# The router of a transformer block on unnormalised rows, in quarters, and the first experts with fixed rows

## The chip, the core and the metric

The kernel runs on one core of a Trainium2 chip. TensorE (PE) multiplies matrices, VectorE (DVE) and ScalarE (ACT) work on rows and on what PE leaves in its accumulator banks (PSUM), GpSimd (POOL) does simple row operations, and the queue of SyncE (SP) issues most transfers. Each engine works through its own list of instructions in order; semaphores make it wait for the others. The metric is the device time of one execution in microseconds (us); less is better.

## The reference, cut to what matters

One encoder block over 512 tokens of width 1024: differential attention and a short convolution are mixed by gates, then a residual, a LayerNorm, a two-level mixture of experts and a second LayerNorm. The change touches the part from `w_o` to the first experts:

```python
mix = (g_a * y_a + g_b * y_b) @ w_o
x = layer_norm(DEEPNORM_ALPHA * x + mix, ln1_g, ln1_b)
g_prob = softmax(x @ w_group + b_group)            # 4 groups, the best is taken
sub_logits = einsum('td,gde->tge', x, w_sub) + b_sub   # 8 experts in each, the best two
weights = g_p * softmax(s_top)
y_e = (silu(x_e @ w_gate_e[e]) * (x_e @ w_up_e[e])) @ w_down_e[e]   # 32 experts, d_expert 512
x = layer_norm(DEEPNORM_ALPHA * x + sum of weight * y_e, ln2_g, ln2_b)
```

`layer_norm(x, g, b)` is `(x - mean) / sqrt(var + eps) * g + b`. All data is float32. For products of full precision the kernel splits one or both factors into a high and a low part (fp32r) and adds the products.

## The kernel before, in words

The schedule is written out by hand: the order in the source is the order on each engine. Tokens stand in four tiles of 128 (`tt` 0 to 3). SBUF is divided into 22 pages of 1 MB, which are handed out in the order in which their last readers stand in the source.

`o_group(j, tt)` multiplies a token tile by a quarter (256 columns) of `w_o` with 24 matmuls (L286 to L288); DVE adds the residual into `u(tt)` and takes the quarter's statistics (L677, L678). The four quarters of `w_o` are units that are split into parts first (`Unit.split`, L168 on ACT, L169). For the last three units of `w_o` DVE makes the first half of the low part and POOL the second (`prep(..., nc.gpsimd)`).

When a tile's four quarters are done, `layer_norm` normalises it on DVE and applies scale and shift (L107 to L115). `turn_x` transposes the normalised tile on PE (L694) and ACT copies it out (L696); `logits` multiplies it by the 36 router columns (L714); `parts_x` makes `XH` on ACT (L705), `XL` on POOL (L706), and multiplies the tile by alpha on POOL (L708). `gate_steps` is a chain of some 16 small DVE operations from the logits to the table of chosen experts `MEM` (L722 to L757). `rank` (L764 to L766) gives each chosen token its place in its expert's list, `counts` (L793) the length of the lists, `positions` (L777 to L788) the row in the expert's input.

The loop over `NP` = 16 follows. Each `i` stands for two experts (a pair), each `dispatch` for two `i`. `dispatch` compares positions with a row of numbers (L821) and gathers by matmuls with `XH` and `XL` (L905, L906); ACT copies the rows to `XG` (L908, L911). `up(i)` is 8 steps of gate and up products (L944), `act` the nonlinearity, `down` the third product (L971). `combine` adds an earlier pair's rows to `u` (L997 on PE, L999 on DVE). An expert's rows need not be 64: each pair may shift 32 rows from its first to its second expert, which `select` reads from `SEL` into a register of PE. What is over 64 (or 96) rows goes to one expert that is run again at the end.

Weights come by page: `experts.load` issues a page's load on SP when a page is given back, 14 pages ahead of use. Before `up` of the first pair, PE has gathered a half of its input (two of four steps of `dispatch(0)`), and gathers the rest between its steps.

Of the kernel before, what the change touches and what calls it, by code (L numbers as in the profile page):

```python
# [37 lines left out]
def block(ctx: ExitStack, tc, a, out, dump=None, stop=None):  # L38
# [174 lines left out]
    class Experts:  # L213

        def __init__(self):
# [4 lines left out]
            self.order = [(i, kind, n) for i in range(NP)  # L222
# [146 lines left out]
    prm = setup[0:42, 1152:1280]  # L369
# [5 lines left out]
    nc.sync.dma_start(prm[40:42], a["subln_g"].rearrange("o (k p) -> (o k) p", p=128))  # L375
    nc.sync.dma_start(lqk[:, 0], a["lambda_q"])
# [4 lines left out]
    rrow = early.tile([1, 36], F32, name="rrow")  # L381
    nc.gpsimd.dma_start(wr[:, :, 0:4], rows_of(a["w_group"][0]))
# [19 lines left out]
    pcol = early.tile([128, 42], F32, name="pcol")  # L402
    ps = ps_tp.tile([128, 512], F32, name="tp")
    nc.tensor.transpose(ps[:, 0:42], prm, ident[0:42, 0:42])
    nc.scalar.copy(pcol, ps[:, 0:42])
# [170 lines left out]
    onesb = early.tile([128, 128], BF, name="onesb")  # L576
# [11 lines left out]
                   allow_small_or_imprecise_dtypes=True)  # L588
    XH, XL = [], []
# [6 lines left out]
    MEM = early.tile([128, NT, NE], BF, name="mem")  # L596
# [85 lines left out]
    rows, gates = {}, {}  # L682

    def turn_x(tt):

        if tt % 2 == 0:
            XH.append(page(f"xh{tt}", (128, 2, D), F32R))
            XL.append(page(f"xl{tt}", (128, 2, D), F32R))
        x2 = u(tt)
        xt = att.tile([128, KC, 128], F32, name="xt", tag="p", bufs=3)  # L690
        for i in range(2):
            ps = ps_tp.tile([128, 512], F32, name="tp")
            for k in range(4):
                nc.tensor.transpose(ps[:, k * 128:(k + 1) * 128],  # L694
                                    x2[:, (i * 4 + k) * 128:(i * 4 + k + 1) * 128], ident)
            nc.scalar.copy(xt[:, 4 * i:4 * i + 4], ps.rearrange("p (k t) -> p k t", k=4))  # L696
# [615 lines left out]
```

## Time and profile before

| | before |
|---|---|
| median of 3 runs | 1167.73 us (1166.67 to 1167.89) |
| the profiled execution | 1169.97 us, its span 1168.3 us |
| mean granted clock of TensorE | 0.974 |
| busy share of the span | PE 93%, DVE 40%, ACT 23%, POOL 12% |
| bytes moved | 264.89 MB, mean 227 GB/s |

A row of the timeline is: start and duration in us, engine, line and operation, output and inputs, shape, and in brackets how long the engine had been idle and what ended that. The 1.67 us between span and time lie around the profiled instructions. Matmuls overlap, so one lasts longer than the distance to the next. A granted clock of 1.0 is 2.4 GHz, 0.5 is 1.2 GHz.

### The profile page before, as it was taken

The page shows a single profiled execution, that of the slowest core. Times are in us where ns is not written, and L with a number is a line of the kernel's source. Part 1 is how long each engine was busy: PE and PEld are TensorE (multiplying, and loading weights), DVE is VectorE, ACT ScalarE, POOL GpSimd, SP SyncE. Part 2 cuts the span into 40 slices and gives each one's busy share as a digit, 9 for nine tenths or more (in the row PEclk, how much of TensorE's full clock was granted, in tenths as well). Part 3 has the DMA queues.
Part 4 walks back from the last instruction along what each step waited for, and adds up shares of the span by engine and source line. Part 5 has one row for each costly group of instructions (what it writes and reads, how often), then busy time and mean ns, then how long its engine had stood idle before and what let it go on. Part 6 is the DMA issues. An engine that isn't in the chain of part 4 may idle for free. (4 is left out here: it accounts for less than half of the span.)

```text
span 1168.3 us, 17372 instructions
## 1 busy us (share of the span) xinstructions
PE 1088.7 (93%) x7138; PEld 722.7 (62%) x7138; DVE 465.6 (40%) x1020; ACT 271.6 (23%) x478; POOL 135.9 (12%) x117
## 2 busy tenths in 40 slices
PE   5999999989999999999949999999999999999984
PEld 3998877767888888888936443545454545443333
DVE  6621565654344433247881132323232232322326
ACT  3413545743023323323221110111111011110000
POOL 2304322311000000023342000000000000000002
PEclk9999999989999999999969999999999999999997
DMA  9332212122332232343286899999999999999921
GB/s 296 109 118 72 73 37 73 60 68 89 109 109 73 72 109 94 122 143 110 80 352 234 326 408 359 408 402 409 400 409 399 410 406 395 409 407 357 413 79 72
DMA packets 103326, 264.89 MB, mean 227 GB/s; under 512 B 4528, under 2 KB 49644, under 8 KB 102732
## 3 DMA queue, kind: packets, MB, share of 16 engines
q1 hardware_dynamic: 102300, 262.27, 59.9%
q8 instruction: 60, 0.98, 0.3%
q10 hardware_dynamic: 720, 1.31, 0.3%
q0 software_dynamic: 224, 0.15, 0.2%
q14 instruction: 22, 0.18, 0.0%
HBM read 260.30 MB, written 3.41 MB: 226 GB/s over the span
## 5 line engine op out<-in xcount | busy, mean ns | idle before, releaser
L508 PE MATMUL mm<-uth,hi_in 128*128 128x512 f32 x448 | 179.2, 400 | 0.0
L509 PE MATMUL mm<-utl,hi_in 128*128 128x512 f32 x448 | 174.8, 390 | 0.0
L510 PE MATMUL mm<-uth,lo_in 128*128 128x512 f32 x448 | 174.7, 390 | 0.0
L944 PE MATMUL gu<-wg,xg 128*32 128x512 f32 (+1 forms) x1024 | 133.3, 592 | 0.0
L944 PE MATMUL gu<-wu,xg 128*32 128x512 f32 (+1 forms) x1024 | 133.2, 592 | 0.0
L971 PE MATMUL y<-wd,ht 128*32 128x512 f32 (+1 forms) x1024 | 114.9, 601 | 1.4 <-ACT ht L963 1.4
L509 PEld LDWEIGHTS mm<-utl,hi_in 128*128 128x128 f32 x448 | 84.4, 188 | 18.6 <-issue 1.0
L508 PEld LDWEIGHTS mm<-uth,hi_in 128*128 128x128 f32 x448 | 84.4, 188 | 18.4 <-ACT oth L476 0.5
L999 DVE TENSOR_TENSOR u<-u,x 128x512 f32<-128x512 f32 x120 | 75.9, 683 | 49.9 <-PE x L997 49.9
L510 PEld LDWEIGHTS mm<-uth,lo_in 128*128 128x128 f32 x448 | 84.4, 188 | 17.8
L954 DVE SCALAR_TENSOR_TENSOR h<-h,w,gu 128x512 f32<-128x512 f32 x16 | 12.0, 747 | 180.9 <-PE gu L944 180.9
L944 PEld LDWEIGHTS gu<-wu,xg 128*32 128x32 f32 x1024 | 33.1, 110 | 76.8 <-issue 72.6
L944 PEld LDWEIGHTS gu<-wg,xg 128*32 128x32 f32 x1024 | 32.7, 110 | 74.8 <-issue 69.6
L997 PE MATMUL x<-ys,st 128*128 128x512 f32 x240 | 67.1, 405 | 12.3 <-DVE u L999 7.1
L971 PEld LDWEIGHTS y<-wd,ht 128*32 128x32 f32 x1024 | 31.8, 111 | 73.2 <-issue 70.5
L169 POOL TENSOR_TENSOR lo_in<-raw_in,hi_in 128x1024 fp32r<-128x1024 f32 x25 | 59.1, 2384 | 146.9 <-ACT hi_in L168 96.2
L905 PE MATMUL x<-S,xh 128*128 128x256 f32 (+1 forms) x256 | 68.8, 302 | 0.6 <-POOL over L1022 0.6
L168 ACT CAST hi_in<-raw_in 128x1024 fp32r<-128x1024 f32 x64 | 63.6, 1046 | 15.5 <-DVE lo_wa L169 8.9
L906 PE MATMUL x<-S,xl 128*128 128x256 f32 (+1 forms) x256 | 66.2, 292 | 0.0
L980 DVE TENSOR_TENSOR ys<-y,ys 128x512 fp32r<-128x512 f32 x32 | 22.0, 691 | 109.7 <-ACT ys L978 109.7
L169 DVE TENSOR_TENSOR lo_in<-raw_in,hi_in 128x1024 fp32r<-128x1024 f32 x39 | 46.0, 1220 | 46.6 <-ACT hi_in L168 46.5
L997 PEld LDWEIGHTS x<-ys,st 128*128 128x128 f32 x240 | 41.1, 188 | 25.2 <-DVE u L999 13.3
(299 smaller groups left out, 1596.6 us busy)
## 6 DMA issues: line engine op xcount, KB each, us to landing
wg<-in_w_gate_e SPq DMA_DIRECT2D x64, 1024.0 KB, 12.4
wu<-in_w_up_e SPq DMA_DIRECT2D x64, 1024.0 KB, 12.4
wd<-in_w_down_e SPq DMA_DIRECT2D x64, 1024.0 KB, 10.0
raw_in<-in_w_in SPq DMA_DIRECT2D x32, 1024.0 KB, 5.6
raw_wa<-in_w_a_proj SPq DMA_DIRECT2D x4, 1024.0 KB, 5.2
raw_wb<-in_w_b_proj SPq DMA_DIRECT2D x4, 1024.0 KB, 5.0
raw_wo<-in_w_o SPq DMA_DIRECT2D x4, 1024.0 KB, 5.5
u<-in_x SPq DMA_DIRECT2D x4, 512.0 KB, 11.5
```

What stands on the lines that cost most here:

```text
L168: nc.scalar.copy(self.hi[:, k], self.raw[:, k])
L169: eng.tensor_sub(self.lo[:, k], self.raw[:, k], self.hi[:, k].bitcast(F32))
L508: nc.tensor.matmul(ps, unit.hi[:, k, sl], xh(k), start=(k == 0), stop=False)
L509: nc.tensor.matmul(ps, unit.hi[:, k, sl], xl(k), start=False, stop=False)
L510: nc.tensor.matmul(ps, unit.lo[:, k, sl], xh(k), start=False, stop=(k == KC - 1))
L905: nc.tensor.matmul(o, part(XH, tt)[:, sl], r, start=(tt == 0), stop=False)
L906: nc.tensor.matmul(o, part(XL, tt)[:, sl], r, start=False, stop=(tt == NT - 1))
L944: nc.tensor.matmul(t[32 * p:32 * p + 32], disp[i // 2][:, k, base + 32 * p:base + 32 * p + 32], of_rows(w, sel, p), start=(k == 0), stop=( ...
L971: nc.tensor.matmul(Y[hf][32 * p:32 * p + 32], ht[:, f, 32 * p:32 * p + 32], of_rows(w, sel, p), start=(f == 0), stop=(f == 3))
L980: nc.vector.tensor_sub(YS[:, 1, c], y, YS[:, 0, c].bitcast(F32))
L997: nc.tensor.matmul(ps, st[:, tt * 128:(tt + 1) * 128], YS[:, n, c], start=(n == 0), stop=(n == 1))
L999: nc.vector.tensor_add(o, o, ps)
```

## The change

- The router's weights are multiplied by the scale of the first LayerNorm once, early on (`router_weights`), the column sums and the share of the shift go to `wsum` and `rbias`. So `logits` works on the rows before normalisation; `gate_steps` puts mean and deviation in with one more operation.
- `turn_x` and `logits` go by quarters of a tile: a quarter is transposed one `o_group` after its own, and its logits come one later still.
- `norm_x` normalises on ACT without scale and shift; `XL` is made on DVE; scale and shift are applied where gathered rows leave PSUM (`scale_shift`, on ACT, for the first pairs also on DVE). The residual gets scale, shift and alpha in `residual_x` on DVE inside the first pair; POOL multiplies scale and shift (`gb_1`) by alpha once, ahead of the `o_group` loop.
- `rank` and the weights of a tile are asked for later. The loop starts with the pairs 2 and 3 (`sequence`). These have fixed rows, 64 for each expert, so their gather needs ranks alone: `first_slots` and `add_tile` gather tile by tile into four banks that are set to zero first.
- `counts`, `positions`, the transposed positions and the first weights move into `up` of the first pair. Two pages (`XG`, `S0`) are taken ahead of the loop, and one weight page fewer is loaded ahead until the first pair is through.

```diff
+        sequence = [*range(2, NP), 0, 1]
         def __init__(self):
             self.free, self.next, self.tiles = 0, 0, {}
             two = "(h g s) (p k) f -> s h p g k f"
             self.g, self.u = (a[n][0].rearrange(two, h=2, g=2, k=KC) for n in ("w_gate_e", "w_up_e"))
             self.d = a["w_down_e"][0].rearrange("(h g s) (j p) c -> s h p j g c", h=2, g=2, p=128)
-            self.order = [(i, kind, n) for i in range(NP)
+            self.order = [(i, kind, n) for i in self.sequence
                           for kind, n in [(c, n) for n in range(4) for c in "gu"] + [("d", n) for n in range(4)]]
             self.order[-4:] = [("over", c, n) for n in range(2) for c in "gu"] + self.order[-4:] + \
...
-    prm = setup[0:42, 1152:1280]
+    prm = setup[0:58, 1152:1280]
...
+    for i, n in enumerate(("ln1_g", "ln1_b")):
+        nc.sync.dma_start(prm[42 + 8 * i:50 + 8 * i], a[n].rearrange("o (k p) -> (o k) p", p=128))
...
+    xcol = small.tile([128, 2, KC], F32, name="xcol")
+    for i, n in enumerate(("ln1_g", "ln1_b")):
+        nc.gpsimd.dma_start(xcol[:, i], a[n][0].rearrange("(p k) -> p k", k=KC))
...
+    def router_weights():
+        byk = lambda ps: ps[:, 0:288].rearrange("p (k c) -> p c k", c=36)
+        t = att.tile([128, KC, 36], F32, name="wb", tag="p", bufs=3)
+        nc.gpsimd.tensor_tensor(t, wr, pcol[:, 50:58].unsqueeze(2).to_broadcast([128, KC, 36]), op=OP.mult)
+        nc.gpsimd.tensor_tensor(wr, wr, pcol[:, 42:50].unsqueeze(2).to_broadcast([128, KC, 36]), op=OP.mult)
+        for w, to in ((t, None), (wr, wsum)):
+            ps = ps_tp.tile([128, 512], F32, name="tp")
+            nc.tensor.matmul(ps[:, 0:288], ones, w.rearrange("p k c -> p (k c)"))
+            if to is None:
+                nc.vector.reduce_sum(wsum, byk(ps), axis=AX.X)
+                nc.vector.tensor_add(rbias, rbias, wsum)
+            else:
+                nc.vector.reduce_sum(to, byk(ps), axis=AX.X)
+    router_weights()
...
+    rows, gates, norms = {}, {}, {}
+    def turn_x(tt, j):
+        if j == 0:
+            rows[tt] = att.tile([128, KC, 128], F32, name="xt", tag="p", bufs=3)
+        ps = ps_tp.tile([128, 512], F32, name="tp")
+        for k in range(2):
+            nc.tensor.transpose(ps[:, k * 128:(k + 1) * 128],
+                                u(tt)[:, (j * 2 + k) * 128:(j * 2 + k + 1) * 128], ident)
+        nc.scalar.copy(rows[tt][:, 2 * j:2 * j + 2], ps[:, 0:256].rearrange("p (k t) -> p k t", k=2))
+    def logits(tt, j):
+        if j == 0:
+            rows[tt, "logits"] = ps_pv.tile([128, 256], F32, name="pv")
+        for k in range(2 * j, 2 * j + 2):
+            nc.tensor.matmul(rows[tt, "logits"][:, 0:36], rows[tt][:, k, :], wr[:, k, :],
+                             start=(k == 0), stop=(k == KC - 1))
+    def norm_x(tt):
+        steps = norm_steps(stats[tt])
+        mv, rs = next(steps)
+        yield
+        yield from steps
+        nb = work.tile([128, 1], F32, name="ln_nb")
+        nc.vector.scalar_tensor_tensor(nb, mv[:, 0:1], -1.0, rs, op0=OP.mult, op1=OP.mult)
+        norms[tt] = rs, nb
+        yield
+        nc.scalar.activation(u(tt), u(tt), AF.Identity, scale=rs, bias=nb)
+        yield
+    def parts_x(tt):
         if tt % 2 == 0:
             XH.append(page(f"xh{tt}", (128, 2, D), F32R))
             XL.append(page(f"xl{tt}", (128, 2, D), F32R))
-        x2 = u(tt)
-        xt = att.tile([128, KC, 128], F32, name="xt", tag="p", bufs=3)
-        for i in range(2):
-            ps = ps_tp.tile([128, 512], F32, name="tp")
-            for k in range(4):
-                nc.tensor.transpose(ps[:, k * 128:(k + 1) * 128],
-                                    x2[:, (i * 4 + k) * 128:(i * 4 + k + 1) * 128], ident)
-            nc.scalar.copy(xt[:, 4 * i:4 * i + 4], ps.rearrange("p (k t) -> p k t", k=4))
-        rows[tt] = xt
-    def parts_x(tt):
-        x2 = u(tt)
-        xk = x2.rearrange("t (p k) -> t k p", k=KC)
+        xk = u(tt).rearrange("t (p k) -> t k p", k=KC)
         h, l = (part(t, tt).rearrange("t (k p) -> t k p", k=KC) for t in (XH, XL))
         nc.scalar.copy(h, xk)
-        nc.gpsimd.tensor_sub(l, xk, h.bitcast(F32))
-        nc.gpsimd.tensor_scalar(x2, x2, ALPHA, None, op0=OP.mult)
-    def logits(tt):
-        xt = rows[tt]
-        ps = ps_pv.tile([128, 256], F32, name="pv")
-        for k in range(KC):
-            nc.tensor.matmul(ps[:, 0:36], xt[:, k, :], wr[:, k, :], start=(k == 0), stop=(k == KC - 1))
-        rows[tt] = ps[:, 0:36]
+        yield
+        nc.vector.tensor_sub(l, xk, h.bitcast(F32))
+        yield
+    def residual_x(tt):
+        nc.vector.tensor_mul(u(tt), u(tt), g1)
+        nc.vector.tensor_add(u(tt), u(tt), b1)
...
-        nc.vector.tensor_add(L, rows.pop(tt), rbias)
+        rs, nb = norms[tt]
+        nc.vector.scalar_tensor_tensor(L, wsum, nb, rbias, op0=OP.mult, op1=OP.add)
+        yield
+        nc.vector.scalar_tensor_tensor(L, rows[tt, "logits"][:, 0:36], rs, L, op0=OP.mult, op1=OP.add)
...
-        ct = ps_tp.tile([128, 512], F32, name="tp")
+        ct = bank()
...
+        nc.gpsimd.memset(CAP[:, 2 * first:2 * first + 4], 64.0)
...
+    first = experts.sequence[0]
+    XG = page("xg0", (128, KC, 256))
+    S0 = page("s0", (128, NT, 2, 128), F32R)
+    W0 = small.tile([128, 4], F32, name="w0")
+    def first_slots(tt):
+        r = RK[:, tt, 2 * first:2 * first + 4].rearrange("p (i j) -> p i j", j=2)
+        for j, ranks in enumerate((iota2, iota1[:, 0:64])):
+            nc.vector.tensor_tensor(S0[:, tt, :, 64 * j:64 * j + 64], ranks.unsqueeze(1).to_broadcast([128, 2, 64]),
+                                    r[:, :, j:j + 1].to_broadcast([128, 2, 64]), op=OP.is_equal)
+    def dispatch_first():
+        banks = [(ps_lg if i < 2 else ps_mm).tile([128, 512], F32, name="lg" if i < 2 else "mm")
+                 for i in range(4)]
+        for t in banks:
+            nc.tensor.matmul(t, onesb, tri[:, 0:1].to_broadcast([128, 512]), start=True, stop=False)
+        return banks
+    def add_tile(banks, tt):
+        r = S0[:, tt].rearrange("p i s -> p (i s)")
+        for x in (XH, XL):
+            for k in range(KC):
+                o = banks[k // 2][:, (k % 2) * 256:(k % 2) * 256 + 256]
+                end = tt == last and x is XL and k % 2 == 1
+                nc.tensor.matmul(o, part(x, tt)[:, k * 128:(k + 1) * 128], r, start=False, stop=end)
+                if end:
+                    for i in (k - 1, k):
+                        scale_shift(XG[:, i], banks[k // 2][:, (i % 2) * 256:(i % 2) * 256 + 256], i, i % 2)
+    def scale_shift(dst, src, k, vector=False):
+        g, b = xcol[:, 0, k:k + 1], xcol[:, 1, k:k + 1]
+        if vector:
+            nc.vector.tensor_scalar(dst, src, g, b, op0=OP.mult, op1=OP.add)
+        else:
+            nc.scalar.activation(dst, src, AF.Identity, scale=g, bias=b)
     prep(NU, NU - 2, nc.gpsimd)
     experts.load(EARLY)
+    nc.gpsimd.tensor_scalar(gb_1, gb_1, ALPHA, None, op0=OP.mult)
     for tt in range(NT):
         for j in range(4):
             if tt == 0 and j < 2:
                 prep(NU, NU - 1 + j, nc.gpsimd)
             o_group(j, tt)
-            if j == 0 and tt > 1:
-                ratio(tt - 2)
-            if j == 2 and 0 < tt < last:
-                turn_x(tt - 1)
-                parts_x(tt - 1)
-            if j == 2 and tt == last or j == 3 and tt == last - 1:
+            before = 4 * tt + j - 1
+            if before >= 0 and before < 4 * last + 3:
+                turn_x(before // 4, before % 4)
+                if before > 0:
+                    logits((before - 1) // 4, (before - 1) % 4)
+            if tt and j == 0:
+                together(norm_x(tt - 1))
+            if tt and j == 1:
+                cast = parts_x(tt - 1)
+                next(cast)
+                together(gate_steps(tt - 1))
+                ratio(tt - 1)
+                together(cast)
+            if tt > 1 and j == 1:
                 rank(tt - 2)
-            if j == 3 and 0 < tt < last:
-                logits(tt - 1)
-        if tt == last:
-            turn_x(last - 1)
-            parts_x(last - 1)
-            logits(last - 1)
-        layer_norm(u(tt), g1, b1, stats[tt], 4, *([gate_steps(tt - 1)] if 0 < tt < last else []),
-                   *([weight_steps(tt - 2)] if tt > 1 else []))
+                together(weight_steps(tt - 2))
+                first_slots(tt - 2)
     ui += 4
-    experts.load(AHEAD - EARLY)
-    turn_x(last)
-    together(gate_steps(last - 1))
-    logits(last)
-    parts_x(last)
-    ratio(last - 1)
+    experts.load(AHEAD - EARLY - 1)
+    banks = dispatch_first()
+    turn_x(last, 3)
+    add_tile(banks, 0)
+    logits(last, 2)
+    logits(last, 3)
+    together(norm_x(last))
+    add_tile(banks, 1)
     rank(last - 1)
-    together(gate_steps(last), weight_steps(last - 1))
+    first_slots(last - 1)
+    add_tile(banks, last - 1)
+    cast = parts_x(last)
+    next(cast)
+    together(gate_steps(last))
+    rank(last)
+    first_slots(last)
+    together(cast)
+    add_tile(banks, last)
     ratio(last)
-    counts()
-    rank(last)
-    positions()
+    together(weight_steps(last - 1))
     together(weight_steps(last))
     nc.gpsimd.tensor_add(GP, of_pair(G)[:, :, :, 0], of_pair(G)[:, :, :, 1])
     mix.close()
...
-    disp, weight = {}, {}
+    disp = {first // 2: XG}
+    weight = {first + i: W0[:, 3 * i:3 * i + 1] for i in range(2)}
...
-                nc.scalar.copy(XG[:, k], ps[:, 0:256])
-                nc.scalar.copy(over["x"][:, k], ps[:, 256:320])
+                scale_shift(XG[:, k], o[:, 0:256], k)
+                scale_shift(over["x"][:, k], o[:, 256:320], k)
             elif k % 2:
-                nc.scalar.copy(XG[:, k - 1:k + 1], ps.rearrange("p (k s) -> p k s", k=2))
+                for i in (k - 1, k):
+                    scale_shift(XG[:, i], ps[:, i % 2 * 256:i % 2 * 256 + 256], i)
...
+        if sel is None:
+            return t[:, p // 2]
...
+    coming = None
+    sels = {first: None, first + 1: None}
+    steps = up(first, None)
+    advance(steps, 2)
+    counts()
+    positions()
+    advance(steps, 3)
     POS_T = bank()
     for tt in range(NT):
         nc.tensor.transpose(POS_T[0:NP, tt * 128:(tt + 1) * 128], POS[:, tt], ident)
     nc.scalar.copy(POST, POS_T[0:NP])
-    coming = dispatch(0)
-    advance(coming, 2)
-    sels = {0: select(0)}
-    steps = up(0, sels[0])
-    for _ in range(3):
-        advance(coming, 1)
-        advance(steps, 2)
-    advance(coming)
+    ps = bank()
+    for i in range(2):
+        for tt in range(NT):
+            nc.tensor.matmul(ps[:, 2 * i:2 * i + 2], S0[:, tt, i].bitcast(F32), GP[:, tt, first:first + 2],
+                             start=(tt == 0), stop=(tt == last))
+    nc.scalar.copy(W0, ps[:, 0:4])
     adding = None
-    for i in range(NP):
-        if i % 2 == 0 and i + 2 < NP:
-            coming = dispatch(i // 2 + 1)
+    for n, i in enumerate(experts.sequence):
+        after = experts.sequence[n + 1] if n + 1 < NP else None
+        if n % 2 == 0 and n + 2 < NP:
+            coming = dispatch(experts.sequence[n + 2] // 2)
             advance(coming, 1)
-        if i + 1 < NP:
-            sels[i + 1] = select(i + 1)
+        if after is not None and after not in sels:
+            sels[after] = select(after)
         advance(steps)
         h = act(*GU, weight[i])
-        if i == 0:
+        if n == 0:
+            for tt in range(NT):
+                residual_x(tt)
+            experts.load(1)
```

## Rows read from the trace of the kernel before

**Rows 1.** Busy time by stage; columns as the first line says.

```profile
core 0: us, PE busy (x) PEld busy (x) DVE busy (x) ACT busy (x) POOL busy (x), PEclk, DMA share, GB/s
545.00:587.30 42.30, 40.48 (x340) 39.90 (x339) 34.15 (x109) 8.58 (x13) 11.43 (x4) 1.00 0.29 109
...
591.00:613.40 22.40, 6.90 (x39) 5.75 (x40) 19.70 (x67) 4.63 (x10) 13.70 (x10) 0.51 0.83 333
613.40:619.80 6.40, 6.37 (x32) 6.28 (x32) 0.97 (x3) 0.64 (x2) 4.95 (x19) 0.57 0.01 3
619.80:640.10 20.30, 20.30 (x177) 9.56 (x176) 1.43 (x4) 3.81 (x6) 2.32 (x11) 1.00 0.80 296
640.10:1133.00 492.90, 477.38 (x4006) 219.03 (x4002) 133.03 (x229) 56.50 (x113) 0.95 (x1) 1.00 0.97 381
```

**Rows 2.** Busy time between the last load ahead and the loop's first loads.

```profile
609.50:622.60 13.10, 10.18 (x64) 7.61 (x68) 4.21 (x19) 1.75 (x3) 9.06 (x35) 0.64 0.01 4
```

**Rows 3.** Timeline of PE from the last quarter of `w_o` to the first expert.

```profile
587.24 1.04 PE L694 MATMUL tp<-ident,u 128*128 128x128 f32 x8
588.51 1.98 PE L714 MATMUL pv<-wr,xt 128*128 128x36 f32 x16 [0.24 <-ACT xt L696]
...
608.50 0.19 PE L793 MATMUL tp<-mem,onesb 128*128 128x32 bf16 x1 [6.94 <-DVE mem L756]
...
613.43 0.55 PE L905 MATMUL x<-S,xh 128*128 128x256 f32 x1 [0.59 <-POOL over L1022]
...
619.82 1.06 PE L944 MATMUL gu<-wg,xg 128*32 x8
```

**Rows 4.** Timeline of DVE: first and last operation of two chains.

```profile
545.88 0.26 DVE L107 BATCH_NORM_AGGREGATE ln_mv<-ln_st 128x2 f32<-128x24 f32 x1
...
547.89 0.16 DVE L85 TENSOR_TENSOR ln_rs<-ln_i,ln_t 128x1 f32<-128x1 f32 x1
...
596.82 0.19 DVE L722 TENSOR_TENSOR L<-pv,rbias 128x36 f32<-128x36 f32 x1
...
600.48 0.19 DVE L756 TENSOR_TENSOR mem<-oh,oh 128x32 bf16<-128x32 f32 x1
```

**Rows 5.** Groups of POOL by line: xcount, busy us, mean ns, idle before.

```profile
L706 POOL TENSOR_TENSOR xl<-u,xh 128x1024 fp32r<-128x1024 f32 x4 | 11.8, 2954 | 39.7 <-ACT xh L705 39.7
L708 POOL TENSOR_SCALAR u<-u 128x1024 f32<-128x1024 f32 x4 | 11.5, 2868 | 0.4
...
L169 POOL TENSOR_TENSOR lo_wa<-raw_wa,hi_wa 128x1024 fp32r<-128x1024 f32 x2 | 4.7, 2371 | 16.3 <-issue 16.3
```

**Rows 6.** Timeline of POOL, then of PE, in the first token tile.

```profile
534.24 9.18 POOL L169 TENSOR_TENSOR lo_wo<-raw_wo,hi_wo 128x1024 fp32r<-128x1024 f32 x3 [7.96 <-DMA wu<-in_w_up_e]
...
540.12 0.39 PE L288 MATMUL mm<-lo_wo,mth 128*128 128x256 f32 x1 [0.21 <-POOL lo_wo L169]
```

**Rows 7.** Groups of ACT by line.

```profile
L911 ACT COPY xg<-x 128x512 f32<-128x512 f32 x28 | 16.5, 588 | 81.9 <-PE x L906 81.9
...
L705 ACT CAST xh<-u 128x1024 fp32r<-128x1024 f32 x4 | 8.4, 2102 | 0.0
...
L168 ACT CAST hi_wo<-raw_wo 128x1024 fp32r<-128x1024 f32 x8 | 7.8, 1047 | 0.0
...
L1248 ACT ACTIVATE u<-x,nb,rs 128x512 f32<-128x512 f32 x2 | 1.6, 777 | 8.0 <-DVE nb L1267 4.3 <-DVE u L1255 3.7
```

**Rows 8.** Groups of DVE by line.

```profile
L169 DVE TENSOR_TENSOR lo_wb<-raw_wb,hi_wb 128x1024 fp32r<-128x1024 f32 x8 | 9.4, 1222 | 9.3 <-ACT hi_wb L168 9.3
...
L677 DVE SCALAR_TENSOR_TENSOR u<-u,mm 128x256 f32<-128x256 f32 x16 | 6.6, 412 | 8.4 <-PE mm L288 7.2 <-PE tp L765 1.2
```

**Rows 9.** Busy time of PE at two pauses; then PEclk, DMA share, GB/s.

```profile
1131.80:1134.00 2.20, 0.00 (x0) 1.00 0.03 7
1134.00:1135.00 1.00, 0.00 (x0) 0.64 0.00 0
...
700.00:702.50 2.50, 0.63 (x3) 1.00 1.02 408
```

More of the change, by code (lines that the diff above doesn't have):

```diff
@@ L399, in block @@
     v_group(1, 3)
-    pcol = early.tile([128, 42], F32, name="pcol")
+    pcol = early.tile([128, 58], F32, name="pcol")
     ps = ps_tp.tile([128, 512], F32, name="tp")
-    nc.tensor.transpose(ps[:, 0:42], prm, ident[0:42, 0:42])
-    nc.scalar.copy(pcol, ps[:, 0:42])
+    nc.tensor.transpose(ps[:, 0:58], prm, ident[0:58, 0:58])
+    nc.scalar.copy(pcol, ps[:, 0:58])
     nc.vector.tensor_scalar(pcol[:, 40:42], pcol[:, 40:42], 1.0 - LAM_INIT, None, op0=OP.mult)
@@ L575, in block @@
     tri = early.tile([128, 128], BF, name="tri")
-    onesb = early.tile([128, 128], BF, name="onesb")
+    onesb = small.tile([128, 128], BF, name="onesb")
     nc.gpsimd.memset(onesb, 1.0)
@@ L595, in block @@
     POST = small.tile([NP, S], BF, name="post")
-    MEM = early.tile([128, NT, NE], BF, name="mem")
+    MEM = small.tile([128, NT, NE], BF, name="mem")
     CNT = small.tile([128, NE], F32, name="cnt")
@@ L775, in positions @@
         A, B = of_pair(RK)[:, :, :, 0], of_pair(RK)[:, :, :, 1]
-        ta, tb, tc_, td = (work.tile([128, NT, NP], F32, name=f"pos{i}", bufs=1) for i in range(4))
+        big = mw.tile([128, NT, 384], F32R, name="S", bufs=1).bitcast(F32)
+        ta, tb, tc_, td = (big[:, :, i * NP:(i + 1) * NP] for i in range(4))
         nc.gpsimd.tensor_scalar(ta, A, 32.5, -64.0, op0=OP.is_gt, op1=OP.mult)
@@ L867, in block @@
         dump("g", G.rearrange("p t e -> p (t e)"), 0)
-        dump("pos", POS.rearrange("p t e -> p (t e)"), 0)
-        dump("cnt", CNT, 0)
     mix.close()
@@ L891, in dispatch @@
         disp[j] = XG
-        more = j == NP // 2 - 1
+        more = 2 * j == experts.sequence[-2]
         if more:
@@ L1012, in block @@
     NO = small.tile([1, 1], I32, name="no")
-    OVER = small.tile([128, NT, NE], F32, name="over")
     PASS = small.tile([128, 1], F32, name="pass")
@@ L1054, in next_pass @@
         each = ind.unsqueeze(1).to_broadcast([128, NT, NE])
-        nc.vector.tensor_tensor(big, OVER, each, op=OP.mult)
+        nc.vector.tensor_sub(big, RK, CAP.unsqueeze(1).to_broadcast([128, NT, NE]))
+        nc.vector.tensor_tensor(big, big, each, op=OP.mult)
         nc.vector.reduce_sum(PLACE[:, 0], big, axis=AX.X)
@@ L1124, in other_pass @@
                 nc.tensor.matmul(o, part(XL, tt)[:, sl], SO[:, tt, 0:64], start=False, stop=(tt == NT - 1))
-        nc.scalar.copy(x, ps.rearrange("p (k s) -> p k s", k=KC))
+        for k in range(KC):
+            scale_shift(x[:, k], ps[:, k * 64:(k + 1) * 64], k)
         ht = turn(act(*up_over(x, w), over["w"][:, 0:1]))
@@ L1164, in block @@
                                           skip_runtime_bounds_check_because="the number of an expert")
-        if i:
-            st = rows_of(i - 1)
+        if n:
+            st = rows_of(before)
             adding = combine(st, YS)
-        if i == NP - 1:
+        if n == NP - 1:
             gb_2 = page("gb_2", (128, 2, D))
@@ L1174, in block @@
             advance(adding, 3)
-        if i < NP - 1:
+        if n < NP - 1:
             ht = turn(h)
         advance(adding, 2)
-        if i % 2:
+        before = i
+        if n % 2:
             advance(coming)
-        if i < NP - 1:
+        if n < NP - 1:
             down(i, sels[i], ht)
-        if i == NP - 2:
+        if n == NP - 2:
             npass = nc.values_load(NPASS[0:1, 0:1], min_val=0, max_val=16)
             tc.mark_branch_hint_location("other passes", hint=(npass > 1), engines=[PE])
-        if i < NP - 1:
+        if n < NP - 1:
             YS = parts_y(Y)
-            steps = up(i + 1, sels[i + 1])
-    last_rows = rows_of(NP - 1)
+            steps = up(after, sels[after])
+    last_rows = rows_of(i)
     YO = over["st"][:, 2:4]
@@ L1196, in block @@
         h2 = act(*gu, over["w"][:, 0:1])
-        down(NP - 1, sels[NP - 1], ht)
+        down(i, sels[i], ht)
         y = down_over(turn(h2), over_w)
@@ L1203, in block @@
     with some.Else():
-        down(NP - 1, sels[NP - 1], turn(h))
+        down(i, sels[i], turn(h))
     YS = parts_y(Y)
-    last_rows = rows_of(NP - 1)
+    last_rows = rows_of(i)
     last_banks = [*GU, *(bank() for _ in range(4)), *Y]
```

11 lines of the change are left out of this document (5 added, 6 removed).

## The prediction

> **What bounds the kernel now.** I began with the busy time by stage [rows 1]. Before 587.3 PE is the bound: 40.5 of 42.3 us busy, with DVE close behind (34.2). From 591.0 to 613.4 PE is busy for 6.9 of 22.4 us at a clock of 0.51, while DVE is busy for 19.7: here the router's chain sets the pace. From 619.8 on PE is busy again for 97% of its time.
>
> The timeline of PE says where the gap begins and ends [rows 3]. The last product with `w_o` ends at 587.24, when the transposes of tile 2 start. The wait of 6.94 us ahead of the counts is for `MEM`, the end of DVE's chain. The gather starts at 613.43 and the first expert at 619.82. So 32.6 us lie between the last product with `w_o` and the first expert, and this is what the change is after.
>
> Is an earlier start worth its full time? From 609.5 to 622.6 the transfers stand still (share 0.01) with the weights loaded ahead [rows 2]: the first expert waits for its rows, not its weights. In the loop PE is the busier side (477.4 of 492.9 us, transfers 0.97) [rows 1]. So I count an earlier first expert one for one.
>
> **Part 1, `router_weights`: +1.0 us.** Two f32 products of 288 columns among the matmuls of an earlier stage, where PE has no time to spare. Eight f32 transposes of 128 columns take 1.04 us, so 576 columns take 0.6; an f32 product of the router shows two instructions for each of its 8 steps [rows 3], which makes 1.2. I take 1.0. POOL's two products and DVE's sums run on engines with time to spare; the four more small transfers at the start I put at nothing, and at 1 us if the start waits for them.
>
> **Part 2, alpha times `gb_1` on POOL: +7.8 us.** This stands in POOL's list between the halves of `w_o`'s second and third unit. All of PE's later work is queued behind the product that waits for them. POOL makes three halves in one piece of 9.18 us from 534.24, and PE waits for the second until 540.12 [rows 6]. A tile of 128x1024 times alpha takes POOL 2.87 us [rows 5]; `gb_1` is twice as wide: 5.7 us. The second half would start at some 537.0; with the scaling ahead it starts at 542.7, takes 2.4 (the rate of the halves of `w_a`) and is ready at 545.1, the third at 547.5.
>
> PE has then been idle for some 4.6 us. After 1131.8 a pause of PE took the clock to the lower level (0.64 on average from 1134.0 to 1135.0), a pause of two us at 700 left it [rows 9]; so I take it that it falls. After 613.43 it stayed low for some 5.5 us: a mean of 0.57 over 6.4 us [rows 1]. A matmul comes every 0.12 us at the upper level (340 in 40.5 us), every 0.22 at the lower. From 545.1: 12 matmuls 2.6, a quarter's transposes and logits 1.0, 12 matmuls 2.6, then 12 at the upper level 1.4: 552.7. Before, 12 from about 543.5 end at 544.9. Without the fall it would be +4.9.
>
> **Part 3, tiles 1 to 3: +3.4 us.** PE has 96 matmuls (11.5), eight transposes (1.04) and the logits (1.98 [rows 3]) per tile, 14.5; with all of it inside this stage three tiles are 43.6. DVE has per tile four quarters (0.8 with their statistics; L677 alone is 0.41 [rows 8]), the deviation (2.2 and one operation), the gate chain (3.85 for 16 operations, 0.24 each [rows 4], with the new one 4.1), `XL`, and eight small operations of ranks, weights and slots (1.9).
>
> `XL` on DVE is not in the trace. The same subtraction on rows that lie together takes 1.22 us [rows 8], the lower end. Here the rows are read with a step of 8 elements. ACT takes 2.10 us for such a copy and 1.05 for one without the step [rows 7]; twice 1.22 is 2.44, the upper end. POOL's own ratio for this subtraction is 2.95 to 2.37 [rows 5], which makes 1.5. I take 1.8, between the two. Then DVE has 13.4 us per tile, less than PE, but 7.8 of it (gate, `XL`, small ones) in one piece ahead of the third quarter's eviction. PE can go on for two `o_group`s in that time (7.3 with transposes and logits) before it lacks a bank or a transpose's input; I add 0.7 per tile for that: 45.8. Before it was 42.4 (544.9 to 587.3). The last product now ends at 587.3 + 7.8 + 3.4 = 598.5.
>
> The Trainium skill speaks against this place of the subtraction: "SBUF — State Buffer", section "Door 1: The DMA port swizzle", says that an access which moves on to another line of 16 bytes pays a penalty, and a step of 8 floats does so each time. ACT's rows above agree with it. By that rule alone `XL` is at its upper end, and the sum is 2.5 us more.
>
> **Part 4, from the last product to the first expert: -15.4 us.** What PE and DVE still have to do in turn: wait for the third quarter's eviction 1.3; transposes, logits of a quarter, four matmuls that zero the banks, transposes 1.9; gather of tile 0 (16 matmuls) 1.9; two quarters' logits 1.0; tile 1 1.9; rank, its eviction and slots of tile 2 1.2; gate chain of tile 3 4.1 (the gather of tile 2 beside it); rank and slots 1.2; `XL` 1.8; two matmuls and the copy out 0.8 (an activation of 512 columns takes 0.78 [rows 7], of 256 I take 0.5). Sum 17.1, so the first expert starts at 615.6 instead of 619.8; before, this way took 32.5. What is gone: applying scale and shift on DVE, POOL's subtraction of 2.95 and scaling of 2.87 [rows 5], and the gather of three tiles after the last rank.
>
> **Part 5, inside the first pair: -3.2 us.** Between 619.8 and 640.1 PE still gathers half the input: 32 matmuls, 3.8 us. That is gone. The transposed positions (0.5) and counts (0.2) come in. Positions take DVE and POOL about 3 us after the counts; three steps of `up`, 5.2 us, lie beside them.
>
> **At nothing.** `residual_x`: eight operations on 128x1024, about 1.22 each [rows 8], 9.8 us on DVE right behind the first `act`. PE then has the next gather, a transpose and `down` before DVE's next result is needed; DVE is busy 27% in the loop [rows 1]. Uncovered it would cost its length once. Normalising on ACT (about 1.6) runs beside the gate chain. `XG` and `S0` take two pages, so each load of weights stands two pages, one `o_group`, later; the first expert's weights start when the units of `w_o` are given back, some 12 us ahead of the first expert, and at 381 GB/s [rows 1] a page of 1.05 MB comes every 2.8 us, ahead of its use.
>
> Sum: 1.0 + 7.8 + 3.4 - 15.4 - 3.2 = **-6.4 us**. The profiled execution goes from 1169.97 to 1163.6, the median from 1167.73 to **1161.3**.
>
> **Rivals.**
> *Clock and subtraction kind (25%).* The clock stays up in the first tile (-2.9), or `XL` costs 1.22 (-1.7, since the piece that delays each eviction and the last chain are shorter): 1157 to 1160. For it: the 4.6 us of idling are close to what rows 9 leave open.
> *The subtraction at double price, or the clock low at the first expert (18%).* `XL` at 2.44 adds 2.5. Between the gather of tile 2 and that of tile 3 PE has little to do for some 4 us; if the clock falls there, up to 5.5 us at half speed cost 2.7: 1163.5 to 1166.5.
> *Slower: ACT's copies in the loop (6%).* Each of 28 copies of 512 columns (0.59) becomes two activations of about 0.5 [rows 7]. If PE waits for each, 0.41 x 28 = 11.5 us, 1173. It decides once 16 of 28 are exposed. Against it: ACT is busy 11% there, PE has four banks.
> *The weights become the bound (5%).* They start 11.2 us later (parts 2 and 3); what was a pause of 13.1 us shrinks to about 2. If the loop ends with the stream, nothing is won: 1168. Against it: PE is the busier side.
> *The last tile's chain is as long as ever (4%).* The gate chain still has to follow the last quarter; if the handovers between engines on its way, some 30, each take 0.2 us more than I count, the gain is gone: 1167 to 1170.
>
> **How the numbers follow.** The forecast has 42%, 1160 to 1163.5 as its own range. The ends: 1161.3 - 2.9 - 1.7 - 1 (scaling and router at their lower prices, rounding) = 1155.5 and 1161.3 + 2.5 + 2.7 + 0.6 = 1167; **1155 to 1167**, which leaves the slower rival and half of the last two out. A change under 0.2%, 2.3 us, can't be told from none. Faster than 1165.4: 42 + 25 + 13 = 80%; slower than 1170.1: 8%; between: 12%.
>
> **What would show it.** Of parts 2 and 3: PE waits for POOL's `lo_wo` in the first tile until about 545, and the last product with `w_o` ends near 598. Of part 4: no big POOL work behind it, and the first `up` 17 us later. Of part 5: `up` of the first pair without gather matmuls between its steps. Wrong it would be if POOL's scaling did not hold up the halves, if `XL` left its bounds, or if the loop from 640 to 1133 changed its length by more than a few us.

## The result, and the profile after

The changed kernel is slower: 1174.31 us median against 1167.73 us, ratio 1.0066 (95% interval 1.0042 to 1.0089). The forecast was 1161.3 us, range 1155 to 1167, with 8% for slower. The profiled execution took 1180.23 us; the five others took 1172 to 1175, and this one is longer in good part because the granted clock was at its lower level (0.5) in more of the first expert (below).

The stages of the changed kernel, cut where its order of work changes:

```profile
core 0: us, PE busy (x) PEld busy (x) DVE busy (x) ACT busy (x) POOL busy (x), PEclk, DMA share, GB/s
...
545.00:560.10 15.10, 14.09 (x102) 14.09 (x103) 4.46 (x17) 1.41 (x4) 3.29 (x2) 0.82 0.00 1
560.10:602.70 42.60, 38.14 (x310) 37.54 (x310) 31.80 (x120) 15.82 (x27) 0.00 (x0) 0.96 0.30 115
602.70:618.50 15.80, 11.69 (x85) 10.45 (x83) 9.90 (x40) 5.32 (x9) 0.00 (x0) 0.90 1.02 409
618.50:636.90 18.40, 18.40 (x153) 6.47 (x153) 7.06 (x30) 2.30 (x6) 8.75 (x36) 0.90 0.72 281
636.90:651.00 14.10, 4.54 (x40) 4.30 (x36) 10.19 (x9) 3.60 (x7) 0.00 (x0) 0.83 0.81 323
651.00:660.50 9.50, 9.49 (x64) 2.46 (x68) 0.00 (x0) 0.57 (x1) 0.00 (x0) 0.72 0.50 163
660.50:1139.00 478.50, 464.59 (x3882) 212.70 (x3878) 132.37 (x228) 66.08 (x130) 0.95 (x1) 0.99 0.98 386
```

The router's gap of [rows 1] is mostly filled: in the last 15.8 us ahead of the first expert PE is busy for 11.7, and counted from the last product with `w_o` (599.96) for 12.5 of 18.5 us. A new hole stands behind the first expert's `up`: PE is busy for 4.5 of 14.1 us. The timeline of ACT, then DVE, then PE shows it:

```profile
637.51 0.60 ACT L1054 ACTIVATE h<-gu 128x512 f32<-128x512 f32 x1
648.55 1.93 ACT L913 ACTIVATE xg<-x,xcol 128x256 f32<-128x256 f32 x4 [10.45 <-issue]
650.36 0.59 ACT L1064 COPY ht<-x 128x512 f32<-128x512 f32 x1
...
638.14 0.75 DVE L1055 SCALAR_TENSOR_TENSOR h<-h,w,gu 128x512 f32<-128x512 f32 x1 [9.25 <-ACT h L1054]
638.80 1.22 DVE L760 TENSOR_TENSOR u<-u,gb 128x1024 f32<-128x1024 f32 x1
...
647.24 1.23 DVE L761 TENSOR_TENSOR u<-u,gb 128x1024 f32<-128x1024 f32 x1
...
640.84 0.60 PE L1062 MATMUL x<-ident,h 128*128 128x128 f32 x4
651.01 9.71 PE L1072 MATMUL y<-wd,ht 128*32 128x512 f32 x64 [9.57 <-ACT ht L1064]
```

PE transposes `h` at 640.84, but ACT, which has to copy it out, first has four copies of the next gather in its list, and these start at 648.55, 0.08 us after the last of the eight operations of `residual_x` (638.80 to 648.47). "issue" names no releaser; the coincidence points to `residual_x`, and `other_page` below tests it. `down`, once free, takes 9.71 us at the lower clock instead of 7.07.

Of part 2, the timeline of POOL, then of PE, in the first tile (before: [rows 6]):

```profile
534.80 2.49 POOL L169 TENSOR_TENSOR lo_wo<-raw_wo,hi_wo 128x1024 fp32r<-128x1024 f32 x1 [7.95 <-DMA wu<-in_w_up_e]
537.38 6.26 POOL L918 TENSOR_SCALAR gb<-gb 128x2048 f32<-128x2048 f32 x1
543.60 4.70 POOL L169 TENSOR_TENSOR lo_wo<-raw_wo,hi_wo 128x1024 fp32r<-128x1024 f32 x2
...
546.01 0.58 PE L291 MATMUL mm<-lo_wo,mth 128*128 128x256 f32 x1 [5.16 <-POOL lo_wo L169]
```

The scaling stands between the halves as forecast (6.26 us, 5.7 expected), and PE waits 5.16 us (4.6 expected). Behind that wait the granted clock is 0.50 from 544 to 550 us, as forecast.

### The profile page after: what moved, and what is told of

Its sections match the earlier page's. It is cut to its first block, busy times and chain, and to the rows that moved or that the text cites. A ratio compares the mean times of both kernels' runs of the same rounds, so it can differ in the third digit from the quotient of the medians.

```text
span 1178.5 us, 17390 instructions
## 1 busy us (share of the span) xinstructions
PE 1095.8 (93%) x7145; PEld 725.4 (62%) x7146; DVE 470.3 (40%) x1036; ACT 290.5 (25%) x514; POOL 119.2 (10%) x116
## 5 line engine op out<-in xcount | busy, mean ns | idle before, releaser
L1072 PE MATMUL y<-wd,ht 128*32 128x512 f32 (+1 forms) x1024 | 117.5, 612 | 10.2 <-ACT ht L1064 10.2
L519 PEld LDWEIGHTS mm<-uth,hi_in 128*128 128x128 f32 x448 | 84.1, 188 | 18.3 <-ACT oth L487 0.5
L1055 DVE SCALAR_TENSOR_TENSOR h<-h,w,gu 128x512 f32<-128x512 f32 x16 | 11.9, 747 | 187.9 <-PE gu L1045 178.6
L1003 PE MATMUL x<-S,xh 128*128 128x256 f32 (+1 forms) x224 | 59.1, 298 | 0.0
L1004 PE MATMUL x<-S,xl 128*128 128x256 f32 (+1 forms) x224 | 57.0, 287 | 0.0
```

What stands on the lines that cost most here:

```text
L519: nc.tensor.matmul(ps, unit.hi[:, k, sl], xh(k), start=(k == 0), stop=False)
L1003: nc.tensor.matmul(o, part(XH, tt)[:, sl], r, start=(tt == 0), stop=False)
L1004: nc.tensor.matmul(o, part(XL, tt)[:, sl], r, start=False, stop=(tt == NT - 1))
L1072: nc.tensor.matmul(Y[hf][32 * p:32 * p + 32], ht[:, f, 32 * p:32 * p + 32], of_rows(w, sel, p), start=(f == 0), stop=(f == 3))
```

## The experiments

The kernel before, run beside them, had medians of 1168.62 us (first four experiments), 1168.46 (next four) and 1167.69 us (last three). The upper level of the granted clock is 1.0, the lower 0.5.

**after_again.** The changed kernel, unaltered. 

> The changed kernel, unaltered, for a second profile of it. The profiled execution took 1180.23 us, the five others 1172 to 1175. If that one was stretched at places where the clock fell by chance, this profile shows 1173 to 1176, with the same stall of ACT from 638 to 648.5 us (some 10 us) and a difference of some 5 us in stretches of low clock; if the profiler itself costs it, it shows 1180 again.

1174.93 us, ratio 1.0066 [1.0043, 1.0089]; six executions from 1173.64 to 1180.15, the one profiled 1175.07. The stall is the same, as expected; here are ACT and PE:

```profile
645.17 1.93 ACT L913 ACTIVATE xg<-x,xcol 128x256 f32<-128x256 f32 x4 [10.45 <-issue]
...
647.63 8.71 PE L1072 MATMUL y<-wd,ht 128*32 128x512 f32 x64 [9.57 <-ACT ht L1064]
```

Its first `up` came at the upper level (17.2 us from start to `h`, against 19.0), and `down` took 1.0 us less. So some 3 of the 5 us between the two executions are the clock at the first expert. Two of the six executions took 1179.5 and 1180.15 us, and neither was the profiled one: such a time does not need the profiler.

**other_page.** By the theory tested here, the first `xg` of the loop gets the page of `gb_1`, scale and shift (no view of the profile shows addresses). Pages go round in the order in which they are given back; `residual_x`, which reads `gb_1`, stands ahead of the first write to `xg` in the source, and so does the extra load. The edit moves the load behind that write:

```diff
                 residual_x(tt)
-            experts.load(1)
...
-        for _ in range(2):
+        for k in range(2):
             advance(coming, 1)
+            if n == 0 and k == 0:
+                experts.load(1)
             advance(adding, 3)
```

Then `xg` should get the page of a block that `up` has read, and the load that of `gb_1`. 

> The first gather inside the loop writes its rows to the page of a weight block that `up` has just read, and the next load of weights takes the page of scale and shift instead; residual_x stays where it is, eight operations of 1.22 us on DVE right behind the first `h`. Theory (the page): ACT waited only because the gathered rows were to stand on the page of scale and shift, which residual_x was still reading. Then ACT copies out at 638 to 639, `down` of the first pair starts some 1.5 us behind its transposes (near 642.5 instead of 651.0), and the time falls by 8.5 to 11 us, to 1163.5 to 1166. Rival 1 (DVE's length itself holds PE or ACT by another wait, or ACT waits for its instructions): no change, 1173 to 1176. Rival 2 (the load that now has to wait for residual_x holds up the stream of weights behind it): half of the gain is lost, 1168 to 1171, and `up` of a later pair shows waits for weights.

1165.18 us, ratio 0.997 [0.9959, 0.9981]: 9.8 us less than `after_again`. ACT, PE, and then SyncE's waits (us in total, times, longest):

```profile
634.82 1.02 ACT L913 ACTIVATE xg<-x,xcol 128x256 f32<-128x256 f32 x2 [1.01 <-PE x L1004]
...
638.29 7.07 PE L1072 MATMUL y<-wd,ht 128*32 128x512 f32 x64 [1.15 <-ACT ht L1064]
```

```profile
SPq L239 <- DVE u L761: 11.9, 1, 11.9
```

`residual_x` runs as before, from 634.51 to 644.18, and holds nobody but a load: ACT copies beside it, `down` starts at 638.29 at the upper level. The wait went with the page, to SyncE: a load now waits 11.9 us for the last operation of `residual_x`, and in `after_again` none does. There it costs nothing: pages are loaded 13 ahead of use, and neither PE nor its weight loads wait more than 0.3 us for weights behind it. The order of ACT's and DVE's work is the same in both kernels, so the theory of the page holds; both rivals fall.

**no_scaling.** POOL's scaling goes, and `residual_x` multiplies by alpha itself:

```diff
-    nc.gpsimd.tensor_scalar(gb_1, gb_1, ALPHA, None, op0=OP.mult)
...
-        nc.vector.tensor_mul(u(tt), u(tt), g1)
-        nc.vector.tensor_add(u(tt), u(tt), b1)
+        nc.vector.scalar_tensor_tensor(u(tt), u(tt), ALPHA, g1, op0=OP.mult, op1=OP.mult)
+        nc.vector.scalar_tensor_tensor(u(tt), b1, ALPHA, u(tt), op0=OP.mult, op1=OP.add)
```

> The product of scale and shift with alpha on POOL is taken out; residual_x multiplies by alpha in its own two operations (three inputs instead of two, same rows). Theory (part 2 of the prediction): the 6.3 us in POOL's list hold the halves of the third and fourth unit of w_o, and with them PE; the first tile's last product ends near 545 instead of 552.9, the time falls by 6 to 8.5 us, to 1166 to 1168.5. Rival: DVE's half of the same units and the eviction of the quarters would have held PE almost as long; a fall of 0 to 2 us, 1172 to 1174.5.

1171.24 us, ratio 1.0024 [1.0013, 1.0035]: 3.7 us less than `after_again`, outside what either theory gave. POOL and PE:

```profile
533.10 9.15 POOL L169 TENSOR_TENSOR lo_wo<-raw_wo,hi_wo 128x1024 fp32r<-128x1024 f32 x3 [7.96 <-ACT hi_wo L168]
...
535.64 0.38 PE L291 MATMUL mm<-lo_wo,mth 128*128 128x256 f32 x1 [0.57 <-POOL lo_wo L169]
...
609.68 1.94 PE L1044 MATMUL gu<-wg,xg 128*32 128x512 f32 x8
```

Up to the first expert the theory holds: from the first product with `w_o` it is 81.4 us instead of 88.2, the 7 us of part 2. But this profile has the first expert at the lower level (1.94 us for eight matmuls, not 1.07) and `down` at 9.68: `up` and `down` lose 2.7 us to the clock, against `after_again`. Why the clock is low there no run shows; of the twelve profiles of the changed kernel and its variants, five have the first expert's first eight matmuls at 1.94 us.

**both.** The two edits together. 

> The page and the scaling together. If the two losses are apart in time and neither covers the other, the sum: 14.5 to 19 us less than the changed kernel, 1155 to 1160, that is 8 to 12 us below the kernel before. If an earlier first expert runs into its weights (they start only when the units of w_o are given back), the sum falls short: 1161 to 1165, with waits of the first `up` for weights.

1158.0 us, ratio 0.9922 [0.9895, 0.9948]: 16.9 us less than `after_again`. That is more than 9.8 and 3.7: here the first expert ran at the upper level (1.06 us for eight matmuls), in the profile of `no_scaling` at the lower. The losses are apart in time, and no wait for weights above 0.3 us took their place.

**spread.** On top of both; the calls for one tile move apart:

```diff
                 ratio(tt - 1)
+            if tt and j == 2:
                 together(cast)
-            if tt > 1 and j == 1:
+            if tt > 1 and j == 3:
                 rank(tt - 2)
```

> On top of the kernel with both repairs (page and scaling; 1158.0 us): per tile the gate chain stays behind the second quarter, the subtraction of XL moves behind the third and ranks, weights and slots behind the fourth, so that a quarter's eviction stands between them on DVE. Theory (part 3: the three in one piece of 7.8 us held the third quarter's eviction, and PE ran out of banks): tiles 1 to 3 take 43.6 to 45 us instead of 49, the last product with w_o is followed at once by its transposes, and the time falls by 4 to 6.5 us, to 1151.5 to 1154. Rival (DVE's total or the clock sets the pace of a tile, the piece only shifts the wait): tiles 1 to 3 stay above 47.5 us, the time falls by less than 1.5 us.

1152.29 us, ratio 0.9868 [0.9839, 0.9897], 5.7 us less than `both`. An eviction is DVE's addition of a finished bank to `u` (L708), which PE needs for its next transposes. First PE's wait for such an eviction in the changed kernel, then DVE at the end of a gate chain there and in `spread`:

```profile
584.07 0.41 PE L721 MATMUL tp<-ident,u 128*128 128x128 f32 x2 [1.98 <-DVE u L708]
```

```profile
565.04 0.19 DVE L805 TENSOR_TENSOR mem<-oh,oh 128x32 bf16<-128x32 f32 x1
565.22 2.10 DVE L755 TENSOR_TENSOR xl<-u,xh 128x1024 fp32r<-128x1024 f32 x1
567.25 0.40 DVE L708 SCALAR_TENSOR_TENSOR u<-u,mm 128x256 f32<-128x256 f32 x1
```

```profile
555.13 0.19 DVE L805 TENSOR_TENSOR mem<-oh,oh 128x32 bf16<-128x32 f32 x1
555.31 0.41 DVE L708 SCALAR_TENSOR_TENSOR u<-u,mm 128x256 f32<-128x256 f32 x1
556.10 2.08 DVE L755 TENSOR_TENSOR xl<-u,xh 128x1024 fp32r<-128x1024 f32 x1
```

The eviction now stands between chain and subtraction. Tiles 1 to 3 take 43.3 us from eviction to eviction, 47.6 in `both` and 49.1 in the changed kernel. In `spread` PE waits nowhere in them and sets the pace; in `both` and in the changed kernel it waits 0.5, 2.0 and 2.0 us. The 1.5 us between those two are clock (mean granted 1.00 in `both`, 0.97 in `after_again`): code and pauses of this stretch are alike, and in `warm` the code of `both` takes 49.1 at 0.96.

**xl_pool.** On top of both:

```diff
-        nc.vector.tensor_sub(l, xk, h.bitcast(F32))
+        (nc.vector if tt == last else nc.gpsimd).tensor_sub(l, xk, h.bitcast(F32))
```

> On top of both repairs: XL of the first three tiles is made on POOL again, the last on DVE. By the piece theory DVE's piece is 2.1 us shorter in each of three tiles: 2 to 5 us less, 1153 to 1156. Rival: POOL's subtraction (2.95 us in the trace of before) slows DVE's operations beside it, as the halves of w_o showed (3.89 us for DVE's half beside POOL's), and the gain is 0 to 1.5 us.

1164.68 us, ratio 0.9968 [0.9951, 0.9985]: 6.7 us *more* than `both`; even the rival was too mild. (The rival's 3.89 us stood beside POOL's scaling, in the changed kernel; beside POOL's halves DVE's took 2.63 to 2.67.) POOL, then DVE:

```profile
554.21 3.10 POOL L755 TENSOR_TENSOR xl<-u,xh 128x1024 fp32r<-128x1024 f32 x1 [12.32 <-ACT xh L753]
...
554.27 3.08 DVE L800 TENSOR_SCALAR oh<-desc,rw 128x32 f32<-128x32 f32 x1
...
558.35 0.24 DVE L800 TENSOR_SCALAR oh<-desc,rw 128x32 f32<-128x32 f32 x1
```

One small operation of the gate chain, 0.24 us by itself, lasts 3.08 us, as long as POOL's subtraction beside it: DVE is spared 2.1 us of work and stands still for 2.8; the other two tiles show the same (3.02 and 3.07 us). The Trainium skill, "SBUF — State Buffer", section "SBUF: two separate sides", says that GpSimd shares a port pair with those VectorE operations that run in a two-port mode or have two SBUF inputs, that the one which starts first holds it for the whole instruction, and that the other blocks. These rows agree; that this operation is of such a kind no row shows. Beside POOL's scaling in the changed kernel (recorded from 537.38 to 543.64 us) DVE's half of a unit ran from 539.07 to 542.96, so there a hold to the end of the instruction is not shown.

Not all of the 6.7 us is this. PE's pauses in tiles 1 to 3 grow by 2.2 us, from 4.5 to 6.7, and the tiles by 5.2, from 47.6 to 52.8, with the granted clock at 0.93 on average instead of 1.00. In this profile the first `up` (18.3 us, 17.2 in `both`) and the third pair's step (35.9 against 34.5) ran longer too, again at the lower clock, and one of the ten executions took 1158.82 us, as long as `both`.

**warm.** On top of both, products that nobody reads, where PE waits for the last tile:

```diff
+    def keep_busy(n):
+        t = ps_mm.tile([128, 512], F32, name="mm")
+        for i in range(n):
+            nc.tensor.matmul(t, onesb, tri[:, 0:1].to_broadcast([128, 512]), start=True, stop=True)
...
+    keep_busy(8)
     together(gate_steps(last))
     rank(last)
+    keep_busy(4)
```

> On top of both repairs: 8 and 4 products of 512 columns that nobody reads are put on PE where it waits for the last tile's gate chain and slots (some 2 and 0.9 us). If the pause of PE there is what takes the clock down in the last gather and, in part of the executions, in the first expert, the last gather (XL) takes 2 us less in part, the first `up` always comes at 1.06 us for eight matmuls, and the time falls by 1 to 2.5 us, with less spread between executions. If the clock falls for another reason, or these products delay the gather, no change or 0.5 us more.

1158.47 us, ratio 0.9909 [0.988, 0.9939]: not told from `both`. PE in `both`, then in `warm`:

```profile
604.67 0.18 PE L814 MATMUL tp<-mem,tri 128*128 128x32 bf16 x1 [1.86 <-DVE mem L805]
605.77 1.19 PE L903 MATMUL lg<-s,xh 128*128 128x256 f32 x4 [0.92 <-DVE s L886]
```

```profile
605.66 1.91 PE L918 MATMUL mm<-tri,onesb 128*128 128x512 bf16 x8
...
608.85 0.71 PE L903 MATMUL lg<-s,xh 128*128 128x256 f32 x4
...
610.74 0.74 PE L903 MATMUL lg<-s,xl 128*128 128x256 f32 x4 [0.70 <-DVE xl L755]
```

The clock stays up in the last gather (0.71 us for four matmuls instead of 1.19), but the second half then waits for `XL`: 0.5 us are won on the way to the first expert. In all three profiles with these products (here, `spread_warm`, `all`) the last gather ran at the upper level throughout, and in none of the nine others. The first `up` ran at it in these three and in four of the nine others, so what the products do for it is not shown.

**over.** On top of both: POOL subtracts the capacities in place in `count_over`, and `next_pass` reads that.

```diff
+        nc.gpsimd.tensor_sub(RK, RK, CAP.unsqueeze(1).to_broadcast([128, NT, NE]))
         nc.gpsimd.memset(PASS, 0.0)
...
-        nc.vector.tensor_sub(big, RK, CAP.unsqueeze(1).to_broadcast([128, NT, NE]))
-        nc.vector.tensor_tensor(big, big, each, op=OP.mult)
+        nc.vector.tensor_tensor(big, RK, each, op=OP.mult)
```

> On top of both repairs: the subtraction of capacities from ranks goes back to POOL (in place, in the first pair), so the third pair's step has one DVE operation of 0.28 us less ahead of the selection of rows. In two profiles of the changed kernel the distance between the third and fourth `h` was 1.6 to 1.75 us more than before, with a low clock behind the pause. If the operation causes it, this distance returns to 34.1 us and the time falls by 0.3 us (where the clock had not fallen) to 1.8 us; if not, the distance goes on varying between 34.5 and 37 us.

1158.38 us, ratio 0.9907 [0.9876, 0.9938]; no gain, and the distance from the third to the fourth `h` is 35.54 us. The theory falls. PE in the changed kernel, in `over`, and in `both`, third pair's step:

```profile
710.41 2.40 PE L1098 MATMUL x<-ys,st 128*128 128x512 f32 x6 [2.63 <-DVE st L1089]
```

```profile
689.72 2.10 PE L1097 MATMUL x<-ys,st 128*128 128x512 f32 x6 [2.31 <-DVE st L1088]
```

```profile
688.34 1.63 PE L1097 MATMUL x<-ys,st 128*128 128x512 f32 x6 [2.64 <-DVE st L1088]
```

The operation makes the pause 0.3 us longer, but with 2.31 the clock fell (2.10 us for six matmuls) and with 2.64 it did not (1.63). Of eleven profiles with a pause of 2.3 to 2.6 us here, that of before among them, seven show the lower level behind it. What decides between the two stays open.

**late.** On top of page, scaling and spread, the whole chain moves out of that pause:

```diff
-        if n == 2:
-            next_pass()
...
             advance(coming)
+        if n == 2:
+            next_pass()
...
         if n < NP - 1:
             down(i, sels[i], ht)
```

> On top of page, scaling and spread (1152.3 us): in the third pair's step the chain that finds the expert to be run again (some 3.3 us on DVE) moves from ahead of the selection of rows to behind the last sum, right ahead of `down`, in which DVE has 6 us without work. Theory: the 2.63 us for which PE waited there becomes the 1.4 us of the other steps, and the clock doesn't fall behind it; the distance from the third to the fourth `h` goes from 34.5 to 37 us to 32 to 33.5, the time falls by 1.3 to 3 us, to 1149.3 to 1151. Rival: the chain then stands in the way of the parts of the third product, or SyncE waits for the expert's number and the loads behind it come late: no gain, 1152 to 1154.

1147.17 us, ratio 0.9814 [0.979, 0.9838]: 5.1 us less than `spread`, more than expected. The distance is 31.60 us (35.87 in `spread`), as in a later pair's step (31.59). In the profiles that is 4.3 us; where the rest of the gain lies can't be told, since the four executions lie at 1144.6 to 1145.3 and at 1149.0 to 1149.7. PE's sum starts without any wait:

```profile
680.82 1.56 PE L1098 MATMUL x<-ys,st 128*128 128x512 f32 x6
```

**spread_warm.** The edit of `warm` on top of `spread`. 

> On top of page, scaling and spread: the 8 and 4 products on PE in the pauses of the last tile's chain. In the profile of spread the first eight matmuls of the first expert took 1.94 us where 1.06 is the upper level, and its `up` 18.2 us instead of 17.2. If the pauses take the clock down, the last gather and `up` run at the upper level: 0.5 to 2 us less, 1150.3 to 1151.8; if not, 1152 to 1153.

1151.05 us, ratio 0.9857 [0.9839, 0.9875], 1.2 us less than `spread`, as expected in size, though the ranges of the two overlap. The first eight matmuls took 1.06 us.

**all.** `late` and `warm` on top of `spread`. 

> Page, scaling, spread, the later chain and the products in the pauses together. If the gains add up, 1147.5 to 1150.5 us, 17 to 21 us below the kernel before; if the clock's falls come back elsewhere, 1150.5 to 1153.

1145.5 us, ratio 0.9809 [0.9793, 0.9825]: 22.2 us below the kernel before, a little better than the best case expected. Against `late` alone no difference can be told.

## Why the prediction was wrong

Its terms against the profile of `after_again` (1175.07 us), whose time is nearest to the median; before is 1169.97 us. Each row runs from the moment that ends the row above to the start of what it names; "before" and "after" are lengths in us.

| up to | before | after | change | predicted |
|---|---|---|---|---|
| first product with `w_o` | 529.45 | 528.76 | -0.7 | +1.0 (part 1) |
| last eviction of tile 0 | 15.51 | 22.76 | +7.3 | +7.8 (part 2) |
| last product with `w_o` | 42.16 | 46.67 | +4.5 | +3.4 (part 3) |
| first expert | 32.70 | 18.78 | -13.9 | -15.4 (part 4) |
| its `down` | 25.64 | 30.66 | +5.0 | -3.2 (part 5) |
| second `h` | 20.02 | 21.66 | +1.6 | 0 |
| end | 504.49 | 505.78 | +1.3 | 0 |
| sum | | | +5.1 | -6.4 |

**The step that failed** is the first under "At nothing": that PE "has the next gather, a transpose and `down` before DVE's next result is needed". No result of DVE was needed; a *page* was. The copy-out of that very gather writes to the page of `gb_1`, which `residual_x` still reads, and ACT has `ht` behind it in its list, and PE `down` behind that. The price that stood beside it ("uncovered it would cost its length once", 9.8 us) is what came: 8.4 us in the fifth row, where `other_page` has 22.24 instead of 30.66, and 1.6 in the sixth, 20.02 there, by the lower clock after the hole; 9.8 us between the medians. That the two agree so well is partly luck: 8.4 us are the part of `residual_x` that stayed uncovered, the rest is clock. With the page alone put right, the kernel takes 1165.18 us, inside the forecast's range. The prediction did count pages, but only for the loads of weights; it did not ask which page the next `XG` would get. A trace of the kernel before could not show it; the order of giving back has to be followed in the source.

**What held.** Part 2: the wait and its length; `no_scaling` gives the 7 us back. The clock fell behind that wait, as the forecast took it, so the rival of a clock that stays up falls. Part 5: with the page moved, 22.24 instead of 25.64, -3.4. Part 4 held in its mechanism and, but for 1.5 us, in its size. ACT's two copies in place of one cost nothing in the loop (second to third `h`: 30.92 us, before 30.88), and no wait for weights above 0.3 us appeared, so the slower rivals of ACT's copies and of the weights both fall; the loss came from a place that no rival named.

**What was mis-sized.** Part 3: the piece of DVE's work that stands ahead of the third quarter's eviction was priced at 0.7 us per tile, 2.1 in all (its sum, 43.6 + 2.1, is 45.7, not 45.8). `spread` shows that without it the tiles run at PE's pace, near the 43.6 taken for PE alone, 4.3 us shorter than in `both` and 5.8 than in the changed kernel. `XL` took 2.05 to 2.11 us, 1.8 taken, bounds 1.22 and 2.44. The rule of the Trainium skill named there gives no figure; with ACT's doubled time it meant the 2.44, and the runs lie between 1.8 and that. Part 4: 18.8 instead of 17.1 us, of which 0.9 is the same piece (2.2 us until PE sees the last tile's third quarter, 1.3 expected), 0.3 is `XL`, and the rest is mostly the last gather at the lower clock, which the prediction had named among its rivals. Part 1's four matmuls took about 1 us at their place (0.40 each), but the start of `w_o` varied from 527.0 to 530.0 in the profiles, so that its net cost stays open. Part 5 adds up to -3.1 from its own terms, not -3.2. The last 1.3 us: `next_pass`, with the clock that falls behind its pause in some executions. One DVE operation was put there by the change, and the prediction passed over it; `over`, which takes it out, did not bring the old length back.

## What to carry to other kernels

Work that is moved "behind" something is free only if nobody waits for its results *and* nobody waits for the storage that it reads: where buffers go round, follow the freed buffer to its next writer, and see what is queued behind that writer. Long chains of small operations on one engine are better split, with the evictions that another engine needs between them; here that was worth 4.3 us. When a repair wins more or less than its stage, look at the clock behind each remaining pause.

## What the runs showed of the hardware

A DVE operation on 128x32 took 3.08 us beside POOL's subtraction, 0.24 by itself. DVE's half of a unit took 3.89 us beside POOL's scaling and 2.63 to 2.67 beside POOL's halves, instead of 1.22 [rows 8]. XL's subtraction, with a step of 8 floats, took DVE 2.05 to 2.11 us instead of 1.22. Pauses of PE of the same length (2.64 us) left the granted clock at the upper level in one profile and took it to the lower in another; in three profiles with products that nobody reads, placed in PE's pauses, the gather behind them ran at the upper level, in nine without them it fell.
